# Swapping two products of a seven-product matmul and rounding weights one item further ahead, in a two-layer decoder trunk

## The chip, the cores and the metric

The kernel runs on one core of a Trainium2 chip. The metric is the device time of one launch in microseconds (us). Times are medians of several runs; a profiled execution gives the trace. In the profile PE is TensorE's matmuls, PEld its weight loads, DVE is VectorE, ACT is ScalarE, POOL is GpSimd and SP is SyncE, which here only issues DMAs.

## The reference

Two layers on 512 tokens of width 1024, in float32. Each layer has a half-step FFN, a mixer (a gated linear recurrence and a sliding-window attention, joined by two sigmoid gates) and a second half-step FFN. Only the FFN and the gates of the mixer meet the change:

```python
def swiglu(h, w_gate, w_up, w_down):
    return (jax.nn.silu(h @ w_gate) * (h @ w_up)) @ w_down

for l in range(DEPTH):
    h = rms_norm(x, gn[0])
    x = x + 0.5 * rms_norm(swiglu(h, w_ffn1_gate[l], w_ffn1_up[l], w_ffn1_down[l]), gn[1])
    ...
    mixed = jax.nn.sigmoid(gate_a) * y_hg + jax.nn.sigmoid(gate_b) * y_at
    x = x + rms_norm(mixed @ w_out[l], gn[3])
    h = rms_norm(x, gn[4])
    x = x + 0.5 * rms_norm(swiglu(h, w_ffn2_gate[l], w_ffn2_up[l], w_ffn2_down[l]), gn[5])
```

The FFN's inner width is 2816, which is 22 blocks of 128.

## The kernel before

**Rounding and three matmuls.** TensorE is fed fp32r operands. Each float32 operand is split into a rounded part `hi` and the rest `lo`, and a product is three matmuls: hi x hi, hi x lo, lo x hi (`mm3`, called by `wmm` for a block of weights). All matmuls are recorded on one line, L115.

**Seven products.** Two blocks of weights (128 gate columns and 128 up columns, or two blocks of gate columns in the mixer) times all 512 tokens can be seen as a product of 2 x 2 quarters: the weights' two halves of the width 1024, and the activations' two halves of the width by two halves of the tokens. `sevenths` computes it with seven quarter products instead of eight, from sums of quarters. One quarter product is four blocks of 128 by three matmuls of 256 columns, so twelve matmuls; one use of `sevenths` is 84. The results go to the PSUM tiles `p1`, `p26`, `p57` (pool `acc`, five buffers) and `p43` (pool `aux`, three buffers); `p43` holds product 4 in its first 256 columns and product 3 in its last. Afterwards DVE joins them in the tile `m` (one buffer) and in `v`: L875 and L877 after product 6, L882 and L883 after the last product. ACT copies product 1 out on L865.

**The loop `fast`** goes through the blocks of an FFN: in the first FFN from block 7, in the other three from block 4, to block 21. Each turn calls `sevenths`, applies the SiLU on ACT (L895) and multiplies on DVE (L896). `early`, in the last turn, rounds the first four results for `down`, the product with `w_down` that follows. Together the four loops make 69 turns; `branches`, in the two mixers, makes 8 more uses of `sevenths`, each followed by blocks of another product.

**Weight items.** `Stream` gives out weights in items. One use of `sevenths` takes four: a (products 1 and 2), b (products 5 and 7), c (products 6 and 4) and d (product 3, half an item). Items b and c are sums of quarters that DVE forms (L312 and L313, L318 and L319) in a tile `tt` with two buffers. `Stream.split` makes an item: ACT rounds it into `whi` (L325). For b and c, and for ordinary items, DVE then subtracts for `wlo` (L332). For a and d ACT writes the negative into `wlo` (L329) and POOL issues a DMA that adds the float32 weight to it (L330). `whi` and `wlo` have WS = 6 buffers each. The float32 weights come from memory into `w32`, with four buffers, by DMAs on SP's queue (L244 and, in pieces, L241; L252 for the pieces of `down`'s quarters). A new one is asked for when an old one has been split.

**What sets the order.** PE runs in the order of the program. For the other engines and queues a planner sets the order ahead of time: an instruction's place in the program gives its priority, and the planner's own times say when it is ready. The place where an item's `split` stands in the program comes from `ahead`, which is called from `whole` (take the next item), and from `used` after each block of weights:

```python
def ahead(self):
    while self.done < min(len(self.items), self.cur + 1 + self.most) and self.flight < WS:
        self.split()
```

`cur` counts the items taken, `done` those split, and `flight` those split and not yet used up. `most` is AHEAD = 3 throughout.

**Behind the loop** comes `down`. Its first four items (the first units of `w_down`) are ordinary ones, and are among the items that `ahead` splits in the last turn of `fast`. Then follow quarters of its own seven products (`quarter`, L282 on ACT and L287 on DVE, product 1 first). `down` also rounds activations (`split`, L401 on ACT, L402 on DVE) and forms sums of their quarters (L459 to L466).

Of the kernel before, what the change touches and what calls it, by code (L numbers as in the profile page):

```python
# [36 lines left out]
W32, WS, AHEAD, TAIL, PLAIN, FIRST, EARLY, LATE = 4, 6, 3, 4, 4, 7, 4, 8  # L37
# [8 lines left out]
def trunk(ctx: ExitStack, tc: tile.TileContext, xin, wall, gains, lbT, hgain, sinks, c_dist, c_mask, c_ident, out):  # L46
# [12 lines left out]
    def nm(s):  # L59
        seq[0] += 1  # L60
        return f"{s}_{seq[0]}"

    def big(dt=F32, shape=None):
        return sb.tile(shape or [P, S], dt, tag="s", name=nm("s"), bufs=SLOTS)
# [4 lines left out]
    def acc():  # L69
        return ps.tile([P, S], F32, tag="acc", name=nm("acc"), bufs=5)  # L70

    def aux():
        return ps.tile([P, S], F32, tag="aux", name=nm("aux"), bufs=3)
# [82 lines left out]
    class Stream:  # L156
# [27 lines left out]
        def gates(self):  # L184
# [6 lines left out]
            self.plain(1)  # L191

        def rows(self, kt, fast):


# [183 lines left out]
    ws = Stream()  # L379
# [7 lines left out]
    def wmm(o, b, mv, start, stop, poll=True):  # L387

        mm3(o, b[2:], mv, start, stop)
        ws.used(b)  # L390
        if poll:
            order.poll()
# [217 lines left out]
    class Late(Quarters):  # L610
# [23 lines left out]
        def raw(self, half, i):  # L634
            return [cut(self.src[self.k0 + 4 + k], HALF[half]) for k in range(4)] if i else self.x1

    def down(src, kt, l, n, nxt, fast):


# [209 lines left out]
    H2 = S // 2  # L849

    def sevenths(pre, between=lambda: None):

        def product(o, it, c, n):
            x = pre.operand(n)
            for k in range(4):
                wmm(o, ws.block(it, c + k), x[k], k == 0, k == 3)

        p1, p26, p57, p43 = acc()[:, :H2], acc(), acc(), aux()  # L860
        s, v = big()[:, :H2], big(F32, [P, 2, H2])
        m = sb.tile([P, 4, H2], F32, tag="m", name=nm("m"), bufs=1)
        w = ws.whole()
        product(p1, w, 0, 1)
        nc.scalar.copy(s, p1)  # L865
        product(p26[:, :H2], w, 4, 2)
        between()
        w = ws.whole()
        product(p57[:, :H2], w, 0, 5)
        product(p57[:, H2:], w, 4, 7)  # L870
        c = ws.whole()
        product(p26[:, H2:], c, 0, 6)
        pairs = [p.rearrange("p (i t) -> p i t", i=2) for p in (p26, p57, p43)]

        nc.vector.tensor_tensor(m[:, 0:4:2, :], pairs[0], s.unsqueeze(1).to_broadcast([P, 2, H2]), op=ALU.add)  # L875

        nc.vector.tensor_tensor(v, pairs[1], m[:, 2:3, :].to_broadcast([P, 2, H2]), op=ALU.add)  # L877
        w = ws.whole()
        product(p43[:, H2:], w, 4, 3)
        product(p43[:, :H2], c, 4, 4)  # L880

        nc.vector.tensor_tensor(m[:, 3, :], p57[:, :H2], v[:, 1, :], op=ALU.add)  # L882
        nc.vector.tensor_tensor(m[:, 1:3, :], pairs[2], v[:, ::-1, :], op=ALU.add)  # L883
        return m

    def fast(pre, a, start):
        def early():
            if j == FT - 1:
                for i in range(EARLY):
                    a[i] = split(a[i])  # L890

        for j in range(start, FT):
            m = sevenths(pre, early)
            z = big(F32, [P, 2, H2])
            nc.scalar.activation(out=m[:, 0:2, :], in_=m[:, 0:2, :], func=AF.Silu)  # L895
            nc.vector.scalar_tensor_tensor(z, m[:, 0:2, :], -1.0, m[:, 2:4, :], op0=ALU.mult, op1=ALU.mult)  # L896
            a.append(z.rearrange("p i t -> p (i t)"))

    def ffn(l, n, pre, nxt, halves=True):
        a = []  # L900

        def gated(og, ou):
            z, u = big(), big()
            if first:
                pin(nc.vector.tensor_tensor(z, og, pre.rb, op=ALU.mult))
                nc.scalar.activation(out=z, in_=z, func=AF.Silu)
                nc.vector.tensor_tensor(u, ou, pre.rb, op=ALU.mult)
                nc.vector.tensor_tensor(u, u, z, op=ALU.mult)
            else:
                nc.scalar.activation(out=z, in_=og, func=AF.Silu)  # L910
                pin(nc.vector.tensor_tensor(u, ou, z, op=ALU.mult))
            a.append(u)

        first = isinstance(pre, First)
        o = quad(pre, halves)
        if first:
            o.append(project(pre))
            o.append(project(pre, aux))
            order.until(lambda: pre.rb is not None)
        if not first:  # L920
            pre.sums()
            pre.sums()
        for j in range(2):
            gated(o[2 * j], o[2 * j + 1])
        if first:
            gated(o[4], o[5])
            for j in range(3, FIRST):
                if j > 3:
                    order.until(lambda: pre.laid)
                    pre.sums()  # L930
                if j == 4:
                    pre.sums()
                gated(project(pre), project(pre))
            fast(pre, a, FIRST)
        else:
            for j in range(2, PLAIN):
                pre.sums()
                gated(project(pre), project(pre))
            fast(pre, a, PLAIN)
        return down(a, FT, l, n + 1, nxt, True)  # L940
# [129 lines left out]
    def mixer(l, pre, nxt):  # L1070
# [177 lines left out]
        def branches(get):  # L1248

            v = sevenths(pre)  # L1250
            src = get()
            for i in range(2):
                g = big(F32, [P, 2, H2])
                nc.scalar.activation(out=g, in_=v[:, 2 * i : 2 * i + 2, :], func=AF.Tanh, scale=-0.5 if i else 0.5)
                p = acc()
                for k in range(4):
                    wmm(p, ws.next(), src[k], k == 0, k == 3)
                g = g.rearrange("p i t -> p (i t)")
                nc.vector.scalar_tensor_tensor(g, g, 1.0, p, op0=ALU.add, op1=ALU.mult)
                yield g  # L1260
# [191 lines left out]
```

## Time and profile before

| | us |
|---|---|
| runs | 2100.14, 2100.54, 2103.34 |
| median | 2100.54 |
| profiled execution | 2100.66 |
| its span, first to last instruction | 2098.9 |

The granted clock of TensorE is 0.999 over the span. The four loops lie at about 91 to 241, 755 to 935, 1099 to 1279 and 1793 to 1973 us; `branches` runs at about 592 to 656 and 1630 to 1694 us.

How to read the views: in a timeline or a chain the columns are start, length, engine and line, and in brackets the idle time of the engine before it with what ended it. A row of the stretches has for each engine the busy time and the number of instructions in brackets, then the granted clock, the mean busy share of the DMA engines and GB/s. A row of the waits has the total, the count and the longest. In the groups, the names are those of the tiles, and the three numbers are minimum, median and maximum in ns.

### The profile page before, as it was taken

The page shows a single profiled execution, that of the slowest core. Times are in us where ns is not written, and L with a number is a line of the kernel's source. Part 1 is how long each engine was busy: PE and PEld are TensorE (multiplying, and loading weights), DVE is VectorE, ACT ScalarE, POOL GpSimd, SP SyncE. Part 2 cuts the span into 40 slices and gives each one's busy share as a digit, 9 for nine tenths or more (in the row PEclk, how much of TensorE's full clock was granted, in tenths as well). Part 3 has the DMA queues.
Part 4 walks back from the last instruction along what each step waited for, and adds up shares of the span by engine and source line. Part 5 has one row for each costly group of instructions (what it writes and reads, how often), then busy time and mean ns, then how long its engine had stood idle before and what let it go on. Part 6 is the DMA issues. An engine that isn't in the chain of part 4 may idle for free.

```text
span 2098.9 us, 35207 instructions
## 1 busy us (share of the span) xinstructions
PE 2090.3 (100%) x13549; PEld 1875.3 (89%) x13549; DVE 1550.5 (74%) x2705; ACT 1122.4 (53%) x1899; POOL 154.2 (7%) x188
## 2 busy tenths in 40 slices
PE   9999999999999999999999999999999999999998
PEld 8899988887888999998899998898778989999987
DVE  5877886766776777789587778767687758777884
ACT  6555564456454555556455556554653545555562
POOL 0011000000000011110001110000000000111000
PEclk9999999999999999999999999999999999999999
DMA  8577653312236357774447775632122563677651
GB/s 246 152 181 184 178 157 135 111 61 71 71 101 203 127 122 182 181 198 122 154 114 176 183 181 150 191 120 92 51 81 61 136 193 103 159 182 181 184 160 51
DMA packets 148071, 298.35 MB, mean 142 GB/s; under 512 B 16992, under 2 KB 74816, under 8 KB 147904
## 3 DMA queue, kind: packets, MB, share of 16 engines
q1 hardware_dynamic: 122416, 228.16, 33.2%
q0 software_dynamic: 25344, 67.91, 18.7%
q8 instruction: 106, 1.74, 0.3%
q14 instruction: 61, 0.50, 0.1%
q10 hardware_dynamic: 144, 0.05, 0.0%
HBM read 213.43 MB, written 14.73 MB: 109 GB/s over the span
## 4 chain that ended last, share of the span: by engine, by line
PE 88%; DMA 0%; DVE 0%; ACT 0%; SPq 0%; issue 0%; ACTq 0%
PE acc L115 64%; PE aux L115 22%; PE aux L125 1%; PE acc L125 1%; DMA wlo<-w 0%; DMA w<-wall 0%; SPq L241 0%; DVE s L402 0%; ACT whi L282 0%; DVE s L731 0%; ACT s L600 0%; DVE s L712 0%; DVE s L896 0%; DVE wlo L287 0%; ACT m L895 0%
## 5 line engine op out<-in xcount | busy, mean ns | idle before, releaser
L115 PE MATMUL acc<-s,whi 128*128 128x256 f32 (+1 forms) x4952 | 1059.3, 311 | 0.4 <-ACT whi L325 0.3
L115 PEld LDWEIGHTS acc<-s,whi 128*128 128x128 f32 x4952 | 808.0, 191 | 51.3 <-issue 3.2
L115 PE MATMUL acc<-s,wlo 128*128 128x256 f32 (+1 forms) x2476 | 766.6, 310 | 0.1
L115 PEld LDWEIGHTS acc<-s,wlo 128*128 128x128 f32 x2476 | 472.6, 191 | 25.0 <-DVE wlo L332 0.4
L325 ACT CAST whi<-w 128x1024 fp32r<-128x1024 f32 (+1 forms) x341 | 316.6, 948 | 237.6 <-PE acc L115 95.5
L115 PE MATMUL acc<-whi,s 128*128 128x512 f32 x1264 | 413.6, 393 | 0.1
L325 ACT CAST whi<-tt 128x1024 fp32r<-128x1024 f32 x154 | 161.4, 1048 | 326.5 <-DVE tt L319 184.2
L332 DVE TENSOR_TENSOR wlo<-w,whi 128x1024 fp32r<-128x1024 f32 (+1 forms) x181 | 218.3, 1215 | 151.4 <-ACT whi L325 149.6
L115 PEld LDWEIGHTS acc<-whi,s 128*128 128x128 f32 x1264 | 237.1, 188 | 54.7 <-ACT whi L325 1.6
L332 DVE TENSOR_TENSOR wlo<-tt,whi 128x1024 fp32r<-128x1024 f32 x154 | 188.1, 1221 | 98.8 <-ACT whi L325 98.7
L115 PE MATMUL acc<-wlo,s 128*128 128x512 f32 x632 | 246.4, 390 | 0.0
L115 PE MATMUL aux<-s,whi 128*128 128x256 f32 (+1 forms) x1248 | 230.4, 285 | 0.0
L330 POOL DMA_DIRECT2D wlo<-w x160 | 137.8, 863 | 1258.6 <-ACT wlo L329 704.9
L115 PE MATMUL aux<-whi,s 128*128 128x512 f32 x592 | 196.7, 390 | 0.0
L115 PEld LDWEIGHTS aux<-s,whi 128*128 128x128 f32 x1248 | 195.2, 192 | 1.1 <-issue 0.5
L115 PE MATMUL aux<-s,wlo 128*128 128x256 f32 (+1 forms) x624 | 177.5, 284 | 0.0
L115 PEld LDWEIGHTS acc<-wlo,s 128*128 128x128 f32 x632 | 118.7, 188 | 23.4
L115 PEld LDWEIGHTS aux<-whi,s 128*128 128x128 f32 x592 | 111.1, 188 | 22.8
L329 ACT ACTIVATE wlo<-w 128x1024 fp32r<-128x1024 f32 (+1 forms) x160 | 129.8, 844 | 0.0
L401 ACT CAST s<-s 128x512 fp32r<-128x512 f32 (+1 forms) x164 | 88.4, 580 | 71.5 <-DVE s L460 67.9
L115 PEld LDWEIGHTS aux<-s,wlo 128*128 128x128 f32 x624 | 119.8, 192 | 0.3
L115 PE MATMUL aux<-wlo,s 128*128 128x512 f32 x296 | 115.2, 389 | 0.0
(186 smaller groups left out, 2128.6 us busy)
## 6 DMA issues: line engine op xcount, KB each, us to landing
w<-wall SPq DMA_DIRECT2D x267, 512.0 KB, 3.7
wlo<-w POOLq DMA_DIRECT2D x83, 512.0 KB, 5.5
w<-wall SPq DMA_DIRECT2D x288, 128.0 KB, 3.3
wlo<-w POOLq DMA_DIRECT2D x77, 256.0 KB, 3.3
x_d<-s SPq DMA_DIRECT2D x48, 256.0 KB, 2.1
s<-x_d SPq DMA_DIRECT2D x48, 256.0 KB, 5.5
w<-wall SPq DMA_DIRECT2D x34, 256.0 KB, 3.0
s<-wall SPq DMA_DIRECT2D x64, 128.0 KB, 3.6
```

The lines of the kernel that those rows point to most:

```text
L115: nc.tensor.matmul(o, lhsT, rhs, start=start, stop=stop)
L125: nc.tensor.transpose(o, src, ident)
L325: i = nc.scalar.copy(it.hi[:, c], w[:, c])
L329: nc.scalar.mul(it.lo[:, c], w[:, c], -1.0)
L330: nc.gpsimd.dma_start(it.lo[:, c].bitcast(F32), w[:, c], accum_op=ALU.add)
L332: nc.vector.tensor_tensor(it.lo[:, c], w[:, c], it.hi[:, c].bitcast(F32), op=ALU.subtract)
L401: nc.scalar.copy(hi, src)
```

## The change

In `sevenths` product 4, which uses item c once more, moves ahead of product 3, and item d is taken only then. Item c is therefore used up before d is taken. In `fast`, and only there, `most` is 4 while the loop runs, so that a fourth item beyond the next is split.

```diff
         nc.vector.tensor_tensor(v, pairs[1], m[:, 2:3, :].to_broadcast([P, 2, H2]), op=ALU.add)
-        w = ws.whole()
-        product(p43[:, H2:], w, 4, 3)
         product(p43[:, :H2], c, 4, 4)
+        product(p43[:, H2:], ws.whole(), 4, 3)
...
+        ws.most = AHEAD + 1
         for j in range(start, FT):
             m = sevenths(pre, early)
...
             a.append(z.rearrange("p i t -> p (i t)"))
+        ws.most = AHEAD
```

## The prediction

> **What bounds the kernel now.** The page first: it says which engine never rests.
>
> ```profile
> span 2098.9 us, 35207 instructions
> PE 2090.3 (100%) x13549; PEld 1875.3 (89%) x13549; DVE 1550.5 (74%) x2705; ACT 1122.4 (53%) x1899; POOL 154.2 (7%) x188
> ```
>
> TensorE is without work for 2098.9 - 2090.3 = 8.6 us in all. No reordering of other engines can win more than that. A busy PE could still be a slow PE, so the view of stretches comes next, cut at the four stretches in which the changed loop `fast` runs, with the two in which the mixers' `branches` run it between them. Columns: busy time (and instructions) of PE, PEld, DVE, ACT, POOL, then the granted clock, the DMA share and GB/s.
>
> ```profile
> 91.00:241.00 150.00, 150.00 (x1252) 150.00 (x1252) 115.58 (x163) 87.13 (x122) 24.32 (x29) 1.00 0.75 181
> 592.00:656.00 64.00, 64.00 (x440) 59.77 (x439) 51.11 (x72) 35.16 (x49) 6.02 (x7) 1.00 0.63 166
> 755.00:935.00 180.00, 180.00 (x1502) 180.00 (x1501) 137.62 (x194) 103.60 (x143) 28.41 (x33) 1.00 0.75 181
> 1099.00:1279.00 180.00, 180.00 (x1502) 179.93 (x1501) 137.66 (x194) 103.52 (x143) 28.42 (x33) 1.00 0.75 181
> 1630.00:1793.00 163.00, 163.00 (x991) 146.46 (x989) 117.63 (x191) 85.41 (x144) 8.60 (x10) 1.00 0.50 144
> 1793.00:1973.00 180.00, 180.00 (x1503) 180.00 (x1501) 137.62 (x194) 103.45 (x143) 28.36 (x33) 1.00 0.75 180
> ```
>
> PE has no idle time there at all. Whether it keeps its pace is read from the chain of waits (start, length, what): one turn of the loop is 24 + 60 = 84 matmuls, seven products of twelve.
>
> ```profile
> 861.86 2.88 PE aux L115 x24
> 864.74 7.20 PE acc L115 x60
> 871.94 2.88 PE aux L115 x24
> ...
> 1226.10 2.88 PE aux L115 x24
> 1228.98 7.33 PE acc L115 x60
> 1236.30 2.88 PE aux L115 x24
> ```
>
> A turn takes 871.94 - 861.86 = 10.08 us, 0.12 us a matmul (1.44 us a product), and the chain runs through PE alone. One turn, at 1228.98, took 7.33 instead of 7.20: 0.13 us. That is the only stall that I find inside the four loops. The Trainium skill (Perfetto Trace Analysis, Identifying the Most-Contended Engine) warns that matmul busy time says little about the distance to the roofline and wants the share of LDWEIGHTS. By the 89% of PEld one could hope for 11%, some 230 us (an estimate); in the loops that change, the PEld column is as full as PE's, so that hope has no place here.
>
> What the other engines do meanwhile, on DVE and then on ACT:
>
> ```profile
> 214.37 0.69 DVE L896 SCALAR_TENSOR_TENSOR s<-m 128x512 f32<-128x512 f32 x1 [1.25 <-ACT m L895]
> 217.38 1.23 DVE L332 TENSOR_TENSOR wlo<-tt,whi 128x1024 fp32r<-128x1024 f32 x1 [1.11 <-ACT whi L325]
> 224.57 0.69 DVE L896 SCALAR_TENSOR_TENSOR s<-m 128x512 f32<-128x512 f32 x1 [1.25 <-ACT m L895]
> ...
> 216.30 1.05 ACT L325 CAST whi<-tt 128x1024 fp32r<-128x1024 f32 x1 [1.70 <-DVE tt L313]
> 220.02 1.05 ACT L325 CAST whi<-tt 128x1024 fp32r<-128x1024 f32 x1 [2.67 <-DVE tt L319]
> 220.97 1.57 ACT L325 CAST whi<-w 128x512 fp32r<-128x512 f32 x2
> 222.44 1.57 ACT L329 ACTIVATE wlo<-w 128x512 fp32r<-128x512 f32 x2
> 223.92 0.61 ACT L895 ACTIVATE m<-m 128x512 f32<-128x512 f32 x1
> ```
>
> Here is the one thing that the page hides. From one L896 to the next it is 224.57 - 214.37 = 10.20 us, while PE turns in 10.08. ACT and DVE wait for each other in a ring (DVE 1.25 us for the SiLU, 1.11 us for a copy; ACT 1.70 and 2.67 us for the sums) and lose 0.12 us a turn against PE. The first loop has 22 - 7 = 15 turns and the others 18, so over 17 periods the lag grows to 17 x 0.12 = 2.0 us. The lookahead pays for it. How far it has been used up at the end of the first loop:
>
> ```profile
> 233.56 4.57 DMA wlo<-w
> 238.13 0.02 SPq L241
> ...
> 238.06 0.40 PE L115 MATMUL aux<-s,whi 128*128 128x256 f32 x2
> 238.30 0.28 PE L115 MATMUL aux<-s,wlo 128*128 128x256 f32 x1
> ```
>
> The low part of item d lands at 233.56 + 4.57 = 238.13; the first matmul that reads it starts at 238.30. There are 0.17 us to spare in the last turn, but they suffice.
>
> **The change, part by part.** No instruction is added or taken away: the same matmuls, copies, sums and DMAs, in another order.
>
> *Product 4 ahead of product 3* (all 77 uses of `sevenths`). Item d is wanted one product later, 12 x 0.12 = 1.44 us, so the 0.17 us become about 1.6. Item c is released 1.44 us earlier. The sums behind both products read both halves of p43 and start when the second product ends, as before: 0 us. What it gains is the stalls that late weights cause now: the 0.13 us, and at most what the start of `down` shows below. In the mixers the request for the item four ahead comes 1.44 us later, since it hangs on `whole()` for d. If nothing covered that it would cost up to 8 x 1.44 = 11.5 us; the cover is the 24 matmuls of 512 columns between two uses, and PE has no idle time in 592 to 656 or 1630 to 1793. No reason excludes a gain, but with no idle time it is 0. I take 0, the end that the rows stand at.
>
> *Four items ahead* (the four loops, not the mixers). By the bookkeeping, item a of the turn after next is now asked for in product 3 instead of the next turn's product 1, b in product 1 instead of 5, c in 5 instead of 6, d in 6 instead of 3. The limit of six items in flight allows this only with the swap: without it c and d are both held in product 3. A request only sets a priority; the planner that orders the queues of ACT, DVE, POOL and SP then decides. The priced consequences:
>
> - One more item has to be rounded at each loop's start, for the costliest kind two ACT passes of about 1.05 us, or 1.05 on ACT and 1.23 on DVE. PE has no wait there to lengthen (755 and 1793 begin without idle time): 0 us. If the cover were gone, 4 x 2.3 = 9 us.
> - In the loop the request for b now stands right behind the last work of a turn, so its two sums on DVE may fill the 1.25 us in which DVE waits for the SiLU. That would shorten the ring to about 10.2 - 1.2 = 9.0 us, under PE's 10.08, and the lag would vanish. PE cannot follow below 10.08, so this too is worth only the stalls that there are. The other bound is the rival below.
> - The first rounding of `down`'s product 1 (16 loads of 128 KB ahead of it) may slip ahead of the last turn's sums. There the start of `down` is the place to look:
>
> ```profile
> 245.37 0.69 DVE wlo L287
> 246.06 0.61 DVE s L877
> ...
> 248.47 0.69 DVE s L896
> ...
> 251.25 1.30 DVE s L402 x2
> 252.60 3.92 PE acc L115 x16
> ...
> PEld acc L115 <- DVE s L402: 0.5, 1, 0.5
> ```
>
> DVE's rounding of product 1's weights (L287) holds up the last turn's sum (L877), this the next rounding of activations (L402), and weight loading waits 0.5 us for it. Nothing stands between 0 and 0.5 us to say how much of it an earlier DVE would remove; I take half, 0.25 us. Behind the wait nothing else is queued but the matmuls.
>
> **The sum.** The profiled execution took 2100.66 us, of which 2098.9 are the span and 1.8 lie around it; it stands 0.12 us above the median of 2100.54. 2100.66 - 0.13 - 0.25 = 2100.28; less the 0.12 by which this execution lies above the median, 2100.2 us. With all of 8.6 us won it would be 2092, but the rest of them shows elsewhere:
>
> ```profile
> PE acc L125 <- DVE s L731: 2.9, 1, 2.9
> PE aux L115 <- DVE eps_t L138: 1.1, 1, 1.1
> ```
>
> These are the last transposes and the kernel's first instructions, far from the change. I count a difference under 0.2% (4.2 us) as no change, about what a measurement of this kernel can tell.
>
> **The rivals.**
>
> 1. *The ring gets longer* (slower). With all six buffers taken, the copy of item a at the head of ACT's queue waits for a buffer that PE frees only when product 4 ends, and the SiLU and the copy of product 1 stand behind it on ACT; for the SiLU waits L896, and for that DVE's next sums. For it: ACT takes its queue in order, and the ring is already 0.12 us too long. Against it: ACT is free 1.70 + 2.67 us a turn, and c is freed earlier than now. It decides when the lag eats the slack: 2.0 us that the lag uses now, 0.17 left, and 2.52 us (a quarter turn) from the extra item, 4.7 us, so from 4.7/17 = 0.28 us a turn on, a ring of 10.36. With one copy of 1.05 us more in the ring (11.25), three loops lose 17 x 1.17 - 4.7 = 15 us each and the first 14 x 1.17 - 4.7 = 12: 2157 us. With a third of it (10.55) it is 3 x 3.3 + 1.9 = 12 us: 2112 us.
> 2. *A new wait at the start of `down`* (slower). Loads and rounding of product 1 (and 6) ahead of the last sums: ACT already waits there for a load. For it: the 0.5 us above, in the one place where PE has no slack. Against it: L287 stands ahead of L877 now, so there is little left to slip. One transfer's landing is the price:
>
> ```profile
> 244.02 1.32 ACT L282 CAST whi<-w 128x512 fp32r<-128x512 f32 x2 [0.86 <-DMA w<-wall]
> s<-wall SPq DMA_DIRECT2D x64, 128.0 KB, 3.6
> ```
>
> At 0.86 to 3.6 us for each of the four loops' ends it is 3.4 to 14 us, 2104 to 2115, in the middle 2109; where the ring shortens at the same time, the lag gives up to 2.0 us back at each end.
> 3. *The accumulating DMAs get in DVE's way.* When DVE's idle time is filled, POOL's issue could be held up.
>
> ```profile
> L330 POOL DMA_DIRECT2D wlo<-w x160: 859/859/1154, 32.4 to 1965.7; - x160
> DMA to landing us min/median/max: 3.2/4.8/10.0
> ```
>
> The issue takes 859 ns in the median and 1154 at most, though DVE is over three quarters busy, so its price is under 0.3 us a DMA, inside the 1.6 us that d then has. One landing as late as the worst (10.0 against 4.8) costs 5.2 - 1.6 = 3.6 us: 2101 to 2104. The Trainium skill (SBUF — State Buffer, the "DVE blocks DMA" trap) says that such a DMA is starved of descriptors by DVE's two-port modes; by its 620 against 3100 ns each would come some 2.5 us later (an estimate). Nothing of it is seen in the 160 issues.
> 4. *Faster by more than 4.2 us.* It would need half of PE's idle time, most of which lies at the ends. Only an execution whose DMAs come late, like the 2103.34 among the runs shown, has that to win.
>
> **How the numbers follow.** Forecast, within 0.2%: 0.58, with rival 3 another 0.03. Rival 1: 0.17, most of it over 2110. Rival 2: 0.18, of it 0.03 under 4.2 us and 0.05 over 2110. Rival 4: 0.04. Within 0.2% of the median, 2096.3 to 2104.7, lie 0.58 + 0.03 + 0.03 of rival 2 = 0.64; slower are 0.17 + 0.15 = 0.32; faster 0.04. The likeliest alone is 2099.7 to 2101.5 (no gain and a little of the run's scatter, or all 0.63 us). The range goes down to 2099.0 and up to 2110, past the middle of rival 2; it leaves out 0.11 of rival 1, 0.05 of rival 2 and rival 4, 0.20 in all.
>
> **What would show it.** Right: PE turns of 10.08 us in all loops, no 7.33; the interval between L896 at 10.08 (ring shortened) or 10.20 (only shifted); item d's landing 1.5 us or more ahead of its matmul; no PE wait at the start of `down`. Rival 1 shows as L896 intervals above 10.36 with PE stalls on wlo in the last turns of each loop; rival 2 as PE idle for a microsecond or more behind each loop. Wrong altogether would be PE gaps in the mixers, which I hold to be untouched.

## The result, and the profile after

| | before | after |
|---|---|---|
| median, us | 2100.91 | 2129.06 |
| runs, lowest to highest | 2100.14 to 2103.34 | 2126.28 to 2132.03 |
| profiled execution | 2100.66 | 2128.28 |
| its span | 2098.9 | 2126.5 |
| granted clock, mean | 0.999 | 0.994 |

The ratio is 1.0132, interval 1.0115 to 1.015: the change makes the kernel 28 us slower. (One line fewer in `sevenths` moves the line numbers behind it: the sums of L882 and L883 are L881 and L882 after.)

The page of the changed kernel, and then the waits of its PE (total, times, longest):

```profile
span 2126.5 us, 35286 instructions
PE 2099.6 (99%) x13549; PEld 1880.6 (88%) x13549; DVE 1552.7 (73%) x2705; ACT 1124.6 (53%) x1899; POOL 154.2 (7%) x188
...
PE acc L115 <- ACT s L401: 18.0, 4, 5.0
```

The same 13549 matmuls, 2705 and 1899 instructions on DVE and ACT. PE's busy time has grown by 9.3 us for the same work, and its idle time from 8.6 to 26.9 us; 18.0 us of that have one name that was not in the list before: four waits for L401, ACT's rounding of `down`'s first activations. Four is the number of loops. The chain of waits at the end of the first loop shows what led to one of them (start, length, what):

```profile
240.09 3.21 DMA w<-wall
...
244.08 0.62 ACT whi L282
244.70 0.27 ACT s L865
244.97 0.53 ACT s L401
245.50 0.04 issue
245.54 7.14 PE acc L115 x18
252.68 1.38 PE aux L115 x6
254.06 4.08 PE acc L115 x18
```

A load of `w_down` lands, ACT rounds it (L282, an item of `down`'s product 1), and only then copies product 1 of the last turn (L865) and rounds the activation that PE waits for (L401). ACT's timeline at that place:

```profile
235.48 1.04 ACT L325 CAST whi<-w 128x1024 fp32r<-128x1024 f32 x1
239.40 1.05 ACT L325 CAST whi<-w 128x1024 fp32r<-128x1024 f32 x1 [2.88 <-DMA w<-wall]
240.81 0.62 ACT L282 CAST whi<-w 128x512 fp32r<-128x512 f32 x1 [0.37 <-DMA w<-wall]
242.68 2.02 ACT L282 CAST whi<-w 128x512 fp32r<-128x512 f32 x3 [1.25 <-DMA w<-wall]
244.60 0.37 ACT L865 COPY s<-acc 128x256 f32<-128x256 f32 x1
244.87 2.18 ACT L401 CAST s<-s 128x512 fp32r<-128x512 f32 x4
```

ACT stood idle for 2.88, 0.37 and 1.25 us in front of loads, with L865 and the four L401 behind them in its queue, although their data had long been there (product 1 of this turn was done 10.08 - 1.44 = 8.6 us before the loop's end at 241.3). In the kernel before, the same L865 ran at 234.64 (its first product was out) and the L401 between the copies of weights:

```profile
234.64 0.35 ACT L865 COPY s<-acc 128x256 f32<-128x256 f32 x1
234.89 0.62 ACT L401 CAST s<-s 128x512 fp32r<-128x512 f32 x1
235.41 1.05 ACT L325 CAST whi<-w 128x1024 fp32r<-128x1024 f32 x1
236.36 1.14 ACT L401 CAST s<-s 128x512 fp32r<-128x512 f32 x2
```

The wait itself is 4.3 us at this loop's end. But the first 18 matmuls afterwards take 7.14 us, where 18 of the same pool a little later take 4.08. The granted clock, third column from the end, shows why. Between the rows below it is 1.00 or 0.50; in each of them it changes, so that its mean tells when. The first two rows are the end of the first loop, then two for each of the others:

```profile
244.00:245.00 1.00, 0.00 (x0) 0.00 (x0) 0.97 (x3) 0.94 (x4) 0.00 (x0) 0.65 0.59 169
251.00:252.00 1.00, 1.00 (x5) 0.76 (x5) 1.00 (x3) 0.10 (x1) 0.00 (x0) 0.94 0.93 297
947.00:948.00 1.00, 0.91 (x2) 0.30 (x2) 1.00 (x2) 1.00 (x4) 0.00 (x0) 0.72 0.88 264
950.00:951.00 1.00, 1.00 (x4) 0.76 (x3) 0.96 (x3) 0.00 (x0) 0.00 (x0) 0.57 0.69 208
1295.00:1296.00 1.00, 0.00 (x0) 0.00 (x0) 0.71 (x2) 0.81 (x2) 0.00 (x0) 0.80 1.02 288
1302.00:1303.00 1.00, 1.00 (x5) 0.82 (x4) 0.24 (x2) 0.81 (x2) 0.00 (x0) 0.79 0.70 204
1998.00:1999.00 1.00, 0.00 (x0) 0.00 (x0) 0.80 (x2) 1.00 (x4) 0.00 (x0) 0.87 0.76 208
2002.00:2003.00 1.00, 1.00 (x5) 0.82 (x4) 0.97 (x3) 0.00 (x0) 0.00 (x0) 0.92 0.83 239
```

At the first end PE is empty from 241.27 on. A mean of 0.65 in the row from 244 puts the fall to one half at about 244.3, 3.0 us after the last matmul; the clock came back at about 251.1, 5.6 us after PE had started again. The other ends differ. PE waited 4.28, 4.70, 4.08 and 4.97 us at the four ends; the clock fell 3.0, 5.1, 2.1 and 4.7 us after the last matmul (at the second end only when PE was at work again) and stayed at one half for 6.8, 3.4, 6.8 and 3.4 us. The span grew by 2126.5 - 2098.9 = 27.6 us, on average 6.9 for each loop's end; of this 18.0 / 4 = 4.5 us are the wait, and the other 2.4 (9.3 / 4 = 2.3 by the busy time) are matmuls at half the clock.

In the loops themselves nothing has moved. The two ends of a turn on DVE, the last matmul of the first loop (before, then after) and the one slow turn in the chain:

```profile
214.29 0.69 DVE L896 SCALAR_TENSOR_TENSOR s<-m 128x512 f32<-128x512 f32 x1 [1.24 <-ACT m L895]
224.49 0.69 DVE L896 SCALAR_TENSOR_TENSOR s<-m 128x512 f32<-128x512 f32 x1 [1.24 <-ACT m L895]
...
240.82 0.28 PE L115 MATMUL aux<-s,wlo 128*128 128x256 f32 x1
240.99 0.28 PE L115 MATMUL aux<-s,wlo 128*128 128x256 f32 x1
...
1242.91 7.36 PE acc L115 x60
```

The ring of ACT and DVE still takes 10.20 us a turn, DVE still waits 1.24 us for the SiLU, and the one slow turn is slow here too (7.36 instead of 7.20). PE ends the loop at 240.99 + 0.28 = 241.27, 0.2 us later than before.

### The profile page after: what moved, and what is told of

Read it like the earlier page. It is cut to its first block, busy times and chain, and to the rows that moved or that the text cites. A ratio compares the mean times of both kernels' runs of the same rounds, so it can differ in the third digit from the quotient of the medians.

```text
span 2126.5 us, 35286 instructions
## 1 busy us (share of the span) xinstructions
PE 2099.6 (99%) x13549; PEld 1880.6 (88%) x13549; DVE 1552.7 (73%) x2705; ACT 1124.6 (53%) x1899; POOL 154.2 (7%) x188
## 4 chain that ended last, share of the span: by engine, by line
PE 94%; DMA 3%; issue 1%; SPq 1%; ACT 1%; DVE 0%; ACTq 0%; POOLq 0%
PE acc L115 69%; PE aux L115 23%; DMA w<-wall 1%; PE aux L125 1%; DMA wlo<-w 1%; SPq L241 1%; PE acc L125 1%; DMA s<-xin 0%; ACT whi L282 0%; ACT whi L325 0%; ACT wlo L329 0%; DMA mask<-c_mask 0%; ACT s L401 0%; ACT s L865 0%; DVE s L502 0%
## 5 line engine op out<-in xcount | busy, mean ns | idle before, releaser
L115 PE MATMUL acc<-whi,s 128*128 128x512 f32 x1264 | 419.9, 398 | 18.3 <-ACT s L401 18.0
L401 ACT CAST s<-s 128x512 fp32r<-128x512 f32 (+1 forms) x164 | 87.6, 580 | 71.5 <-DVE s L460 67.9
```

What stands on the lines that cost most here:

```text
L115: nc.tensor.matmul(o, lhsT, rhs, start=start, stop=stop)
L401: nc.scalar.copy(hi, src)
```

## The experiments

What an item's `split` asks for is more than its own rounding. The split of unit 1 of `w_down` frees a buffer of `w32`, and with it `load` asks for the second float32 unit of `down`'s seven products. That unit has a "side": 16 loads (L252) into eight tiles of tag `s`, the tag of nearly all 128x512 tiles. Before, unit 1 was split in product 5 of the last turn, behind the copy of product 1 (L865) and behind `early` (L401); with four items ahead it is split in product 1, in front of both. Three theories stood:

- A: the tiles of tag `s` get their buffers in the program's order, so that L865 and L401 are planned only after the side loads have been placed, and these stand on SP behind the loads of `w_down`.
- B: with the deeper lookahead the copies of weights are simply ranked ahead of L865 and L401 on ACT.
- C: the swap of the products makes item buffers come free in an order that causes the waits.

Each kernel is compared with the kernel before on the same chip.

**The swap alone.**

```diff
-        w = ws.whole()
-        product(p43[:, H2:], w, 4, 3)
         product(p43[:, :H2], c, 4, 4)
+        product(p43[:, H2:], ws.whole(), 4, 3)
```

> Product 4 ahead of product 3, with three items ahead as before. Theory A (in the program the 16 loads of down's side quarters, with their eight tiles of tag s, now stand ahead of the copy of product 1 and of the rounding of down's first activations in the last turn, and these get their tiles only behind them): the swap moves none of this, so 2099 to 2102 us and no PE wait on L401. Theory B (deeper lookahead: the copies of weight items are ranked ahead of those two on ACT, whatever the loads do): also 2099 to 2102. Theory C (the swap itself makes the item buffers come free in another order and causes the waits): 2120 to 2130.

Measured: 2101.4 us, ratio 0.9999 (0.9989 to 1.0008). No wait for L401. C falls, and the swap is worth nothing that shows.

**Four items ahead alone**, with the old order of the products.

```diff
+        ws.most = AHEAD + 1
         for j in range(start, FT):
...
+        ws.most = AHEAD
```

> Four items ahead with the old order of the products. Theory A: the weight unit whose split triggers the side loads is split in product 1 of the last turn as in the changed kernel, so the same four waits of 4 to 5 us on L401: 2122 to 2132 us. Theory B: the same. Theory C: 2099 to 2103.

Measured: 2128.23 us, ratio 1.0126 (1.0111 to 1.0141). Its PE waits:

```profile
PE acc L115 <- ACT s L401: 19.6, 4, 5.6
```

The lookahead carries the whole loss; the swap neither causes nor mends it. The prediction had said that six buffers allow four items ahead only with the swap. By the bookkeeping of `ahead` the old order only moves the request for item a from the start of product 3 to its end.

**The whole change, the side loads later.**

```diff
-                self.side[u + 1] = [pieces(j0 + q, 1) for q in range(4)]
+                self.side[u + 3] = [pieces(j0 + q, 1) for q in range(4)]
```

> The whole change, but the side loads are asked for two units of w_down later, so that in the program they stand behind the copy of product 1 and the rounding of the activations again; the lookahead stays at four. Theory A: no PE wait on L401 behind the loops, 2098 to 2103 us. Theory B: the copies of weights keep their rank, so the waits stay, 2120 to 2132.

Measured: 2101.43 us, ratio 0.9999 (0.999 to 1.0008). ACT's timeline at the end of the first loop:

```profile
235.44 1.04 ACT L325 CAST whi<-w 128x1024 fp32r<-128x1024 f32 x1
236.38 0.36 ACT L865 COPY s<-acc 128x256 f32<-128x256 f32 x1
236.64 1.66 ACT L401 CAST s<-s 128x512 fp32r<-128x512 f32 x3
239.21 1.05 ACT L325 CAST whi<-w 128x1024 fp32r<-128x1024 f32 x1 [0.91 <-DMA w<-wall]
240.16 0.61 ACT L401 CAST s<-s 128x512 fp32r<-128x512 f32 x1
```

The weights are split as early as in the changed kernel, ACT still waits for a load, but L865 and three L401 now stand in front of that wait. B falls. The lookahead of four without the trap gives back all 28 us and wins nothing beyond.

**The kernel before, with `early` behind product 6.** Three items ahead, the old order of the products; only the rounding of activations now stands behind the side loads in the program.

```diff
         product(p26[:, :H2], w, 4, 2)
-        between()
         w = ws.whole()
...
         product(p26[:, H2:], c, 0, 6)
+        between()
```

> The kernel before (three items ahead, old order of products), with one edit: down's first four activations are rounded behind product 6 of the last turn instead of behind product 2, so that the side loads stand ahead of them (not ahead of the copy of product 1). Theory A: PE waits for L401 at the start of down though nothing else has changed, 2 to 5 us and the low clock after it, four times: 2110 to 2130 us. Theory B: the rounding is merely 4.3 us (three products) later in rank with the same lookahead, PE has it in time: 2099 to 2104.

Measured: 2127.61 us, ratio 1.0124 (1.0109 to 1.0139). ACT at the end of the first loop, and PE's waits:

```profile
239.35 1.05 ACT L325 CAST whi<-w 128x1024 fp32r<-128x1024 f32 x1 [3.54 <-DMA w<-wall]
240.84 0.62 ACT L282 CAST whi<-w 128x512 fp32r<-128x512 f32 x1 [0.44 <-PE aux L115]
...
244.85 0.62 ACT L282 CAST whi<-w 128x512 fp32r<-128x512 f32 x1 [0.81 <-DMA w<-wall]
245.37 2.17 ACT L401 CAST s<-s 128x512 fp32r<-128x512 f32 x4
...
PE acc L115 <- ACT s L401: 17.7, 4, 5.1
```

The same loss without the change. ACT was idle for 3.54 us ahead of 239.35 and did not take up the rounding, whose data are the FFN's first four results, made ahead of the loop. With three items ahead the copies L282 belong to items that are asked for only in `down`, so they stand behind the rounding in the program, and yet ACT ran all four of them first (from 240.84 on, L401 at 245.37). A lower rank does not explain that; something else kept L401 back. The time of 2 to 5 us a wait was right at its upper end.

**A tag of their own for the side tiles.** The loads stay where the change puts them in the program.

```diff
-SLOTS = 61
+SLOTS = 54
...
-                        v = [big(), big()]
+                        v = [sb.tile([P, S], F32, tag="side", name=nm("s"), bufs=8) for _ in range(2)]
```

> The whole change, with the side loads at the same place in the program, but their eight tiles have buffers of their own (tag side, 8) and tag s has 54 instead of 61. Theory A in the form that the tiles of one tag get their buffers in the program's order: the copy of product 1 and the rounding no longer stand behind the loads, 2099 to 2103 us and no PE wait on L401. If it is the place of the loads on SP's queue or the transfers themselves that hold ACT up, it stays at 2120 to 2132.

Measured: 2105.99 us, ratio 1.0023 (1.0014 to 1.0032), 3 us above the range expected. ACT behind the first loop, and PE's longest waits:

```profile
236.46 0.36 ACT L865 COPY s<-acc 128x256 f32<-128x256 f32 x1
236.72 1.66 ACT L401 CAST s<-s 128x512 fp32r<-128x512 f32 x3
239.38 1.05 ACT L325 CAST whi<-w 128x1024 fp32r<-128x1024 f32 x1 [1.00 <-DMA w<-wall]
...
PE aux L115 <- ACT s L1059: 3.7, 2, 1.9
```

The waits for L401 are gone. What is left over 2101 are mostly two waits of 1.9 us for L1059, in the mixers, which have 54 buffers here instead of 61 (that this is their cause was not tested).

On SP's queue the loads did not stay. With buffers of their own, the 16 of the first loop are issued between 17 and 42 us, and there are none at the loop's end. So this run does not test the expectation's rival, that their place on the queue or their transfers hold ACT up. What speaks against it are the kernels before and after the change (one line each):

```profile
242.42 7.97 SPq L252 DMA_DIRECT2D s<-wall  x16
241.51 7.67 SPq L252 DMA_DIRECT2D s<-wall  x16
```

The loads run at nearly the same time in both, and in the changed kernel the first was issued only 5 us after ACT had fallen idle at 235.48 + 1.04 = 236.52, with L865 waiting behind.

**The control: 62 buffers in one tag.**

```diff
-SLOTS = 61
+SLOTS = 62
```

> The control for it: the whole change with 62 buffers in tag s, as many in sum as the run with the tag of its own has, and the side tiles among them. If the number of buffers decides, about half way or back to 2100; if their order decides, nothing changes: 2124 to 2132 us.

Measured: 2131.26 us, ratio 1.0138 (1.0121 to 1.0155).

```profile
PE acc L115 <- ACT s L401: 17.3, 4, 4.7
```

As many buffers as in the run before, and the whole loss is back. Nor is it that the side loads snatch the free buffers: if they held eight of 62, the others would have 54, and with 54 they ran without these waits. What is left is the order within the tag: L865 and L401 get no buffer before the side tiles, which stand ahead of them in the program, have theirs. The traces show the order on ACT that comes of it; the planner's own step is inferred from these runs.

**`early` at the start of the last turn**, in the whole change. Only the copy of product 1 is then behind the side loads.

```diff
-            m = sevenths(pre, early)
+            early()
+            m = sevenths(pre)
```

> The whole change, with down's first four activations rounded at the start of the last turn, ahead of the side loads, while the copy of product 1 stays behind them. Theory A: no PE wait on L401 at the start of down; the copy of product 1 comes some 10 us late on ACT, and with it the last turn's sums, so that the next activations come late for down's third unit: PE waits there for 0 to 2 us, too short for a low clock. 2100 to 2110 us. If the copy of product 1 is what PE waits for, 2120 to 2132.

Measured: 2106.83 us, ratio 1.0028 (1.0018 to 1.0038). PE's waits, and the stretch around the first of them:

```profile
PE acc L115 <- ACT s L865: 4.4, 4, 1.3
...
240.00:246.00 6.00, 5.00 (x25) 3.92 (x24) 5.16 (x8) 2.84 (x6) 0.00 (x0) 1.00 0.84 234
```

The time is in the range, the place is not: PE waits directly for L865, which holds the PSUM buffer of product 1, and not for later activations. And with four waits of 1.0 to 1.3 us the clock stays at 1.00.

## Why the prediction was wrong

*What bounds the kernel* was read rightly: PE without a gap, at most 0.6 us to win from the change. The whole change without the trap (side loads later) has a ratio of 0.9999.

*Product 4 ahead of product 3*, costed at 0 us: measured 2101.4 against 2101.55 us. The slack of item d did grow. Its low part lands at 233.48 + 4.28 = 237.76 in the changed kernel, and the first matmul that reads it starts at 239.91:

```profile
233.48 4.28 DMA wlo<-w
...
239.91 0.28 PE L115 MATMUL aux<-s,wlo 128*128 128x256 f32 x1
```

That is 2.15 us instead of 0.17; I had said 1.6. The slow turn that I hoped to see gone stayed, 7.36 us; so the 0.13 us was not won.

*The mixers untouched* held. In the changed kernel PE is full there:

```profile
592.00:656.00 64.00, 64.00 (x416) 58.59 (x415) 51.25 (x75) 34.86 (x49) 6.02 (x7) 1.00 0.54 138
```

*The ring of ACT and DVE*: the shortening to 9.0 us did not come, nor did rival 1's lengthening; it is 10.20 as before. The sums for b have a higher rank, but DVE is as idle before L896 as it was.

*The step that failed* is "the first rounding of `down`'s product 1 (16 loads of 128 KB ahead of it) may slip ahead of the last turn's sums", bounded by 0 and 0.5 us, with rival 2 as its bad end. The place and the mechanism's outline were right: loads and rounding for `down` get in front, ACT waits for landings, PE waits at the start of `down`, and rival 2's sign, PE idle for a microsecond or more behind each loop, is what came. Three things in it were wrong.

- I moved the wrong instructions past each other. I followed the rounding of product 1's weights against the sums behind product 3. What decided was that the 16 side loads, which hang on the split of unit 1, passed the copy of product 1 and `early`. Counting the DMAs that a moved step issues would have found it: from `load`, the unit that has a side is asked for when unit 1 is split, and the change moves that from product 5 to product 1.
- The price. I took one landing, 0.86 to 3.6 us. ACT takes its queue in order, so all four copies behind loads stood in front of PE's operand: 4.1 to 5.0 us each time.
- The clock after it was left out: on average 2.4 us of the 6.9. The Trainium skill (TensorE: Matmul & The Clock Gate, What's actually happening) states that an idle window of about 3.4 us halves TensorE's clock, and that the like of it in work brings it back. The trace agrees in part: the clock was at one half for one or two times that figure (3.4 and 6.8 us), and waits of 1.3 us left it alone, but it fell 2.1 to 5.1 us after the last matmul and came back 3.2 to 5.6 us after the first. Applied to rival 2, whose upper end was 3.6 us of idle time, it would have raised that rival's price.

Four ends at 6.9 us make 2128 us, against 2109 for rival 2. The chance of 0.18 that I gave it was too low: its one argument against, that little was left to slip, looked at DVE's order alone.

## What to carry to other kernels

When lookahead is deepened, follow what each earlier request brings along (loads, and the tiles that they need) past which other requests of the same buffers, above all at the loop's end, where the next stage's items begin. In a program whose buffers are handed out in program order, a load that must wait can hold up a later instruction that has all its data. A wait of TensorE can cost more than its own length: here waits of 4.1 to 5.0 us cost 2.4 more on average, those of 1.0 to 1.9 us none.

## What the hardware showed that I had not expected

That the penalty after a gap outlasts the gap, and does not follow its length. The shortest of the four waits, 4.08 us, was followed by 6.8 us at half the clock, the longest, 4.97 us, by 3.4. In all four runs with the long waits each such spell lasts 3.4 or 6.8 us, and their starts lie 703.1, 348.2 and 703.1 us apart, although the distance between PE's waits differs by up to 1.7 us from run to run. So the clock seems to change only at set times some 3.4 us apart; that is inferred from these spells. Gaps of 1.0 to 1.3 us, and of 1.9 us in the run with a tag of its own, had no effect. Between 1.9 us and the 4.0 us of the shortest wait with an effect nothing was tried in the loops.
